# A second recorded plan for attention, first weights split one stage early, and step-size products moved ahead of the last K tiles

## The chip, the cores and the metric

The kernel runs on one core of a Trainium2 chip. The metric is the device time of one execution in microseconds. A core has five engines with a queue each: TensorE (PE, matmuls; its weight loads are shown as PEld), VectorE (DVE), ScalarE (ACT), GpSimd (POOL) and SyncE (SP), which here only issues DMAs. Each engine runs its own queue of instructions in order, and engines wait for one another by semaphores.

## The reference

One layer of a hybrid decoder on 256 tokens (b = 1, s = 256) of width 2048, all in float32. Cut to what matters:

```python
a_in = _rmsnorm(h, attn_norm_g[i])
proj = a_in @ w_in[i]
z, xbc, dt_raw, q, k, v = jnp.split(proj, [o1, o2, o3, o4, o5], axis=-1)
xbc = jax.nn.silu(_causal_dwconv(xbc, conv_w[i], conv_b[i]))
xs, bm, cm = jnp.split(xbc, [...], axis=-1)
dt = jax.nn.softplus(dt_raw + dt_bias[i])
y = _ssd(xs_h, dt, a_neg, bm, cm)          # chunked state-space scan, 32 heads of 64, 4 groups
...
y_ssm = _rmsnorm(y * silu(z), ssm_norm_g[i])
y_att = _swa_sinks(qh, kh, vh, sinks[i])   # 32 query heads, 8 key heads of 64, window 128, sinks
h = h + jnp.concatenate([y_ssm, y_att], axis=-1) @ w_out[i]
u = _causal_dwconv(_rmsnorm(h, ffn_norm_g[i]) @ w_up[i], ffn_conv_w[i], ffn_conv_b[i])
g_ff, u_ff = jnp.split(u, [D_FF], axis=-1)
h = h + (jax.nn.silu(g_ff) * u_ff) @ w_down[i]
gate = jax.nn.sigmoid(_rmsnorm(h, ple_norm_g[i]) @ w_ple_gate[i])
pe = _rmsnorm(p[i] @ w_ple_proj[i], ple_post_g[i])
h = h + gate * pe
```

## The kernel before

Every large product is made of float32 numbers split in two halves of the type fp32r: hi is the rounded number, lo the rest, and a product is hi*hi + hi*lo + lo*hi. A weight block of 128 x 1024 is loaded by SP into one of 7 raw buffers (`w`), cast by ScalarE to `wh` and subtracted by VectorE to `wl` (`split`, L580 to L584; 4 buffers of each). One such block makes a weight group on TensorE: 12 matmuls of 128 x 512 (2 token blocks x 2 K tiles x 3), into a pair of accumulators `acc`, one for each block of 128 tokens. There are two pairs; a pair can be written again once its reader, an evacuation by ScalarE or `add_to_h` on VectorE (L799, two adds into the residual `h`), has run.

The kernel has four parts:

- **First products** (about 5 to 54 us). For each of 16 K tiles, `first_products` (L732) multiplies the input with two columns of w_in into `acc_b` and `acc_c` (the B and C of the scan), and `dt_products` (L738, L739) adds the step sizes into a bank `ms`. TensorE's order is written by hand. The last two K tiles go column by column, and the step-size products of the last four K tiles stand behind them. The weights of the step sizes (`dhl`) lie in a pool that closes here; the next part uses its space.
- **SSD part** (about 55 to 325 us). A `Recorder` records each instruction with its reads, writes and buffer rings, gives it a duration from a table of costs (`cost`), and a list scheduler (`solve`, six rounds) sets the order on all five engines, which are then issued in that order. All these instructions show the line L280. `x0` to `x3` are the four groups of heads; for each, TensorE forms `ms<-Xd,seg` (within a chunk), `ms<-xe,Bt` (states) and `ms<-prev,CT` (from the state before) between weight groups. `acc_b`, `acc_c` and `dt` enter with given times at which they are taken to be ready.
- **Attention** (about 325 to 600 us). TensorE's order is written by hand: a table `at` says at which weight group (slot) a step is put between the products. The other four engines are ordered by the general tile scheduler, which a few `high_priority` blocks steer. For each of four groups of query heads: evacuate q (L1148), normalise and rotate it, turn it by a DMA transpose, scores (L1221) into `sc`, mask add (L1225), maximum (L1232, L1234), exponentials with their sum (L1237, L1241), `den` (L1242, L1243), scaling (L1246 or L1248), a copy to `half` (L1250), a DMA transpose to `flip` (L1171), GpSimd's copy back to `s` (L1172), values (L1264) into `tr`, and their split to `yh`, `yl`. Three such chains run per group: the first token block at once, the second in two halves. In between run the output products of the SSD groups and of the query groups before, with their `add_to_h`.
- **FFN and gate** (about 600 to 1402 us). A planner of its own (`Plan`) orders all engines. Its first products are those of the layer embedding with four blocks of `w_pe`.

Of the kernel before, what the change touches and what calls it, by code (L numbers as in the profile page):

```python
# [21 lines left out]
P = 128  # L22
T = 256
# [26 lines left out]
GATES_SECOND = (1, 3)  # L50
TURNED = ("by", "xby", "xby", "xby")
# [24 lines left out]
class Ring:  # L76

    def __init__(self, n, at=()):
        self.n, self.at, self.frees = n, at, []
# [17 lines left out]
class Plan:  # L97
# [3 lines left out]
    def __init__(self):  # L101
        self.jobs = []
# [9 lines left out]
    def run(self):  # L112
# [37 lines left out]
        for j in self.jobs:  # L150
            j.ready = j.at
            idle.setdefault(j.engine, 0.0 if j.engine == "PE" else -20.0)
            if not j.need:
                waiting.setdefault(j.engine, []).append(j)
# [95 lines left out]
class Recorder(Plan):  # L250

    def __init__(self, engines, tables):
        super().__init__()
        self.tables, self.open, self.rings = tables, None, {}
        self.V, self.S, self.G, self.PE, self.SY = (Voice(self, *e) for e in engines)
# [4 lines left out]
    def ring(self, pool, tag, n, at=()):  # L260
        return self.rings.setdefault((id(pool), tag), Ring(n, at))

    def keep(self, real, shape, pool=None, tag=None, n=1, at=-20.0):
        t = Lazy(shape, F32, None, real=real)
# [52 lines left out]
    def solve(self, idle, rounds=6):  # L317
        before = [list(j.after) for j in self.jobs]
        pe = [j for j in self.jobs if j.engine == "PE"]
        best = None  # L320
        for _ in range(rounds):
            done = self.simulate(pe, idle, before)
            end = max(j.start + j.dur for j in done if j.engine == "PE")
            if best is None or end < best[0]:
                best = end, done, {j: (j.start, j.late, j.ready) for j in done}
            pe = [j for j in done if j.engine == "PE"]
        self.end = best[0]
        for j in best[1]:
            j.start, j.late, j.ready = best[2][j]
        return best[1]  # L330

    def simulate(self, pe, idle, before):
        for j, a in zip(self.jobs, before):
            j.after = list(a)
            j.late, j.then, j.ready = math.inf, [], j.at
            for r, i in j.slots:
                if i >= r.n:
                    j.after.extend(k for k in r.frees[i - r.n] if k is not j)
                elif r.at:
                    j.ready = max(j.ready, r.at[i])  # L340
# [74 lines left out]
def cost(engine, method, args, kw, outs, ins):  # L415
# [21 lines left out]
    return 0.07 + 0.00107 * n, 0.0  # L437
# [3 lines left out]
def hybrid_layer(  # L441
# [279 lines left out]
    with xin_:  # L721
# [21 lines left out]
        for k in range(KT):  # L743
# [86 lines left out]
    with tc.tile_pool(name="ssd", bufs=1) as sp, tc.tile_pool(name="dram", bufs=1, space=bass.MemoryType.DRAM) as dp:  # L830
        plan = Recorder(zip(("DVE", "ACT", "POOL", "PE", "SP"), real_engines), {AF.Silu, AF.Exp, AF.Ln, AF.Sin})
# [260 lines left out]
        for step in ORDER:  # L1092
# [13 lines left out]
        jobs = plan.solve({"PE": 0.0, "ACT": -4.0, "DVE": -3.0, "POOL": -3.0, "SP": -20.0})  # L1106
# [4 lines left out]
        keys_acc = [t.real() for t in keys_acc]  # L1111
        for lhs, *_ in held.values():
            lhs.t = [(h.real(), l.real()) for h, l in lhs.t]
    sb, (acc_pair, tr_tile, ms_tile), hres, pe_group = eager, real_tiles, real_h, ExitStack
    fill(const)
    by_hand.__exit__(None, None, None)
# [3 lines left out]
    ssh = sb(small, [P, NB, 4], "ssh", bufs=1)  # L1120
    with tc.tile_pool(name="att_s", bufs=2) as as_, tc.tile_pool(name="att", bufs=2, reuse_waits="tile") as ap_, tc.tile_pool(name="ps_sc", bufs=1, space=PSUM) as ps_sc:
        qscaled = sb(as_, [P, HD], "qgs", bufs=1)
# [43 lines left out]
        def flipped(dst, n, put):  # L1166
# [4 lines left out]
            nc.sync.dma_start_transpose(flip, half.rearrange("p a n -> p (a n)"))  # L1171
# [38 lines left out]
        def scores(j, b, kvs):  # L1210
# [5 lines left out]
            sc = ps_sc.tile([P, 2, 2 * NC // (2 * W), W], F32, tag="sc", name=nm("sc"))  # L1216
            for kv in kvs:
                for i in range(2):
                    for e in range(2):
                        es = slice(e * HD, (e + 1) * HD)  # L1220
                        PE.matmul(  # L1221
                            sc[:, e, (kv - kvs[0]) * 2 + i, :], lhsT=qT[es, kv * 2 + i, :], rhs=kT[es, 2 * j + kv, :W], start=True, stop=True
                        )
# [9 lines left out]
            with tc.high_priority():  # L1233
                V.tensor_tensor(out=v3(nm_, 2), in0=v3(nm_, 2), in1=pairs(nsink), op=ALU.min)  # L1234
# [4 lines left out]
            with tc.high_priority():  # L1239
                V.tensor_tensor(out=v3(es_, 2), in0=v3(nm_, 2), in1=pairs(sink), op=ALU.add)  # L1240
                S.activation(out=es_, in_=es_, func=AF.Exp)  # L1241
                V.tensor_tensor(out=den, in0=den, in1=es_, op=ALU.add)  # L1242
                V.reciprocal(den, den)  # L1243
# [10 lines left out]
        def values(j):  # L1254

            yT = Lhs(yp_, KG, "y")
            for b in range(NB):
                o = tr_tile()
                for kv in range(2):
                    pT = probs.pop((j, b, kv))  # L1260
                    vs = slice((2 * j + kv) * HD, (2 * j + kv + 1) * HD)
                    for kb in range(b + 1):
                        for e in range(2):
                            PE.matmul(  # L1264
                                v3(o[e * HD : (e + 1) * HD, kv * 2 * P : (kv + 1) * 2 * P], 2),
                                lhsT=v[kb][:, vs],
                                rhs=pT[e][:, :, kb, :],
                                start=(kb == 0),
                                stop=(kb == b),
                                skip_group_check=True,  # L1270
                            )
# [36 lines left out]
        def embedding():  # L1308
            pt_ = sb(act, [P, KG, T], "ah3")[:, :KW, :]
            nc.scalar.dma_start(pt_, pT)  # L1310
            nc.scalar.dma_start(fcw, ffn_cw)
# [8 lines left out]
        with tc.manual_schedule(engines={PE.engine}):  # L1320
            for part in (
                lambda: q(0),
                lambda: chunk(11, load_v),
                lambda: q(1),
                lambda: output(1),
                lambda: q(2),
                lambda: output(2),
                lambda: q(3),
                *(lambda i=i: output(i) for i in range(3, 8)),
            ):  # L1330
                for _ in part():
                    if slot in at:
                        at[slot]()
                    slot += 1
        fill(as_)
    mix.close()
# [9 lines left out]
    with tc.tile_pool(name="ffn", bufs=2, reuse_waits="tile") as fp:  # L1346

        plan = Plan()
# [116 lines left out]
        def embed(n, ks):  # L1465
            w = weights(w_pe[n, 0])
# [590 lines left out]
```

## Time and profile before

| what | us |
|---|---|
| time, median of 3 runs (lowest, highest) | 1403.42 (1402.94, 1405.18) |
| time of the profiled execution | 1403.67 |
| its span from first to last instruction | 1402.0 |
| TensorE busy in the span | 1387.4 |
| VectorE busy | 1222.8 |
| ScalarE busy | 987.3 |
| GpSimd busy | 129.1 |
| mean granted clock of TensorE (share) | 0.996 |

The profile lists groups of instructions with busy time, mean duration, and the idle time of the engine in front of them with the instruction that ended it. A row of the timeline has the start, the duration, the engine, the line, the operation, output <- inputs, how many alike follow each other, and in brackets the idle time before the row and what ended it. A wait for several semaphores is put down to the one that came last by the profile, which need not be the one that mattered. Matmuls overlap, so the duration of one (0.39 us) is more than the distance to the next (0.23 us).

### The profile page before, as it was taken

How to read it: one execution, taken by the hardware profiler on the slowest of the kernel's cores; microseconds unless marked ns; L12 is line 12 of the kernel's file. 1: busy time of each engine (PE TensorE's matmuls, PEld its weight loads, DVE VectorE, ACT ScalarE, POOL GpSimd, SP SyncE). 2: the span in 40 equal slices, each digit the busy share in tenths (PEclk: the TensorE clock that was granted, in tenths of full speed). 3: DMA queues.
4: the chain of work that ended last, by engine and by line, in shares of the span. 5: the costliest groups of instructions: out<-in, count | busy, mean ns of one | idle time of the engine just before them, and what ended most of it. 6: DMA issues, size and time to landing. Idle time of an engine off the chain costs nothing.

```text
span 1402.0 us, 18224 instructions
## 1 busy us (share of the span) xinstructions
PE 1387.4 (99%) x6307; PEld 1134.1 (81%) x6307; DVE 1222.8 (87%) x1641; ACT 987.3 (70%) x1302; POOL 129.1 (9%) x113
## 2 busy tenths in 40 slices
PE   9999999999999999999999999999999999999998
PEld 7787888888776777888888888888888888888886
DVE  5698877767679898699999999999999999987998
ACT  6687686774666767476787785867687676877763
POOL 0010100018155251000000000000000000000000
PEclk9999999999999999999999999999999999999999
DMA  9576777767686787676887786786877677788563
GB/s 337 211 243 196 210 235 218 206 192 226 182 216 179 213 227 192 203 228 192 253 234 205 228 212 210 206 255 192 232 213 225 214 219 228 198 251 274 169 202 105
DMA packets 189292, 302.57 MB, mean 216 GB/s; under 512 B 116561, under 2 KB 119185, under 8 KB 188945
## 3 DMA queue, kind: packets, MB, share of 16 engines
q1 hardware_dynamic: 188768, 300.95, 72.1%
q8 instruction: 49, 0.80, 0.2%
q10 hardware_dynamic: 432, 0.48, 0.1%
q14 instruction: 43, 0.34, 0.1%
HBM read 270.41 MB, written 4.23 MB: 196 GB/s over the span
## 4 chain that ended last, share of the span: by engine, by line
PE 65%; DVE 1%; DMA 0%; issue 0%; ACT 0%; POOL 0%; DVEq 0%; SPq 0%; POOLq 0%; ACTq 0%
PE b L1433 19%; PE b L1431 19%; PE b L1432 19%; PE acc L620 3%; PE acc L621 2%; PE acc L622 2%; PE tr L1264 1%; PE b L1528 0%; DMA flip<-half 0%; PE sc L1221 0%; DVE wl L584 0%; DVE h L799 0%; PE b L1978 0%; DVE nm L1234 0%; DVE c L1939 0%
## 5 line engine op out<-in xcount | busy, mean ns | idle before, releaser
L1385 ACT CAST wh<-w 128x1024 fp32r<-128x1024 f32 x300 | 314.2, 1052 | 153.3 <-PE b L1433 115.8
L1389 DVE TENSOR_TENSOR wl<-w,wh 128x1024 fp32r<-128x1024 f32 x300 | 361.5, 1220 | 27.4 <-ACT wh L1385 24.9
L584 DVE TENSOR_TENSOR wl<-w,wh 128x1024 fp32r<-128x1024 f32 (+1 forms) x115 | 148.3, 1296 | 55.4 <-ACT wh L583 55.0
L583 ACT CAST wh<-w 128x1024 fp32r<-128x1024 f32 (+1 forms) x115 | 116.6, 1026 | 73.1 <-PE acc L622 61.7
L1431 PE MATMUL b<-wh,gh 128*128 128x512 f32 x398 | 155.0, 389 | 0.0
L1433 PE MATMUL b<-wh,gl 128*128 128x512 f32 x398 | 154.9, 389 | 0.0
L1432 PE MATMUL b<-wl,gh 128*128 128x512 f32 x398 | 154.8, 389 | 0.0
L1433 PE MATMUL b<-wh,al 128*128 128x512 f32 x360 | 140.1, 389 | 0.0
L1431 PE MATMUL b<-wh,ph 128*128 128x512 f32 x352 | 137.2, 390 | 0.0
L1433 PE MATMUL b<-wh,pl 128*128 128x512 f32 x352 | 137.0, 389 | 0.0
L1432 PE MATMUL b<-wl,ph 128*128 128x512 f32 x352 | 136.9, 389 | 0.0
L1431 PE MATMUL b<-wh,ah 128*128 128x512 f32 x344 | 134.0, 390 | 0.0
L1432 PE MATMUL b<-wl,ah 128*128 128x512 f32 x344 | 133.8, 389 | 0.0
L280 DVE TENSOR_TENSOR wl<-w,wh 128x1024 fp32r<-128x1024 f32 x80 | 97.4, 1235 | 29.4 <-ACT wh L280 26.4
L280 PE MATMUL acc<-wh,ah 128*128 128x512 f32 x288 | 116.6, 405 | 0.0
L280 ACT CAST wh<-w 128x1024 fp32r<-128x1024 f32 x80 | 82.9, 1048 | 46.3 <-PE acc L280 42.0
L280 PE MATMUL acc<-wh,al 128*128 128x512 f32 x288 | 112.5, 391 | 0.0
L280 PE MATMUL acc<-wl,ah 128*128 128x512 f32 x288 | 112.4, 390 | 0.0
L620 PE MATMUL acc<-wh,yh 128*128 128x512 f32 x224 | 89.7, 401 | 3.4 <-ACT s L1246 1.9
L621 PE MATMUL acc<-wl,yh 128*128 128x512 f32 x224 | 88.0, 393 | 0.0
L622 PE MATMUL acc<-wh,yl 128*128 128x512 f32 x224 | 87.9, 393 | 0.0
L1433 PEld LDWEIGHTS b<-wh,gl 128*128 128x128 f32 x398 | 74.7, 188 | 15.5
(297 smaller groups left out, 2855.4 us busy)
## 6 DMA issues: line engine op xcount, KB each, us to landing
w<-in_w_up_dram SPq DMA_DIRECT2D x176, 512.0 KB, 4.2
w<-in_w_in_dram SPq DMA_DIRECT2D x126, 512.0 KB, 4.4
w<-in_w_down_dram SPq DMA_DIRECT2D x88, 512.0 KB, 4.4
w<-in_w_out_dram SPq DMA_DIRECT2D x64, 512.0 KB, 4.2
w<-in_w_pg_dram SPq DMA_DIRECT2D x32, 512.0 KB, 3.8
seg<-scr SPq DMA_DIRECT2D x8, 512.0 KB, 6.1
xt<-in_xT_dram SPq DMA_DIRECT2D x16, 128.0 KB, 6.6
h<-in_x_dram SPq DMA_DIRECT2D x2, 1024.0 KB, 8.7
```

The source lines that it names most:

```text
L280: getattr(real, method)(*(concrete(a) for a in args), **{k: concrete(a) for k, a in kw.items()})
L583: S.copy(hi, src)
L584: V.tensor_tensor(out=lo, in0=src, in1=hi.bitcast(F32), op=ALU.subtract)
L620: PE.matmul(acc[b], lhsT=hi, rhs=wh[:, i, :], start=(k == 0), stop=False)
L621: PE.matmul(acc[b], lhsT=hi, rhs=wl[:, i, :], start=False, stop=False)
L622: PE.matmul(acc[b], lhsT=lo, rhs=wh[:, i, :], start=False, stop=(k == total - 1 or (b == NB - 1 and k + 1 == whole)))
L1264: PE.matmul(v3(o[e * HD : (e + 1) * HD, kv * 2 * P : (kv + 1) * 2 * P], 2), lhsT=v[kb][:, vs], rhs=pT[e][:, :, kb, :], start=(kb == 0), st ...
L1385: S.copy(o.h, src.t)
L1389: V.tensor_tensor(out=o.l, in0=src.t, in1=o.h.bitcast(F32), op=ALU.subtract)
L1431: PE.matmul(t, lhsT=hi, rhs=wh, start=first, stop=False)
L1432: PE.matmul(t, lhsT=hi, rhs=wl, start=False, stop=False)
L1433: PE.matmul(t, lhsT=lo, rhs=wh, start=False, stop=last)
```

## The change

1. The step-size products of the last four K tiles now stand ahead of the column-by-column products of the last two.
2. Attention is recorded as well, in a second `Recorder` with the table set {Exp}. Its plan is handed the state of the first one: when each engine comes to rest, and when the buffers of each ring come free (`carry`, `left`, `begun`). The `high_priority` blocks are gone, scores and values become groups on TensorE, the transposes and two loads of ScalarE go through the plan. The FFN's planner starts from the times at which attention's engines come to rest.
3. The first three splits of attention's first weights are made at the end of the SSD list (`AHEAD = 3`), and the four splits of `w_pe` at the end of the attention list.
4. The costs of the plan change: GpSimd's power, two-input and other operations, a ScalarE DMA issue, and a floor of 0.25 for small VectorE operations. `acc_b`, `acc_c` and `dt` are taken to be ready at -2.5, 0.2 and -5.0 instead of -4.4, -1.6 and 0.3.

TensorE, VectorE, GpSimd and SP have the same instructions in another order; ScalarE has one table load more, in the SSD part. TensorE's order in attention and in the FFN is the same as before.

```diff
+AHEAD = 3
...
+        for k in range(KT - 4, KT):
+            dt_products(k)
         for c in range(KW):
             for k in (KT - 2, KT - 1):
                 first_products(k, c)
-        for k in range(KT - 4, KT):
-            dt_products(k)
         by_hand.close()
...
+    if engine == "ACT" and method == "dma_start":
+        return 0.1, 4.0
...
     if engine == "POOL":
-        return 0.4 + 0.0012 * n, 0.0
+        if kw.get("op") == ALU.pow:
+            return 0.6 + 0.16 * n, 0.0
+        return (0.6 + 0.0015 * n if method == "tensor_tensor" else 0.3 + 0.0011 * n), 0.0
...
-    return 0.07 + 0.00107 * n, 0.0
+    return max(0.07 + 0.00107 * n, 0.25 if n <= 8 else 0.0), 0.0
...
-        acc_b, acc_c = ([plan.keep(t, [P, NC], ps_acc, f"acc{b}", 2, at) for b, t in enumerate(acc)] for acc, at in ((acc_b, -4.4), (acc_c, -1.6)))
+        acc_b, acc_c = ([plan.keep(t, [P, NC], ps_acc, f"acc{b}", 2, at) for b, t in enumerate(acc)] for acc, at in ((acc_b, -2.5), (acc_c, 0.2)))
...
-        dt_ps = plan.keep(dt_ps, [P, NC], ps_ms, "ms", 2, 0.3)
+        dt_ps = plan.keep(dt_ps, [P, NC], ps_ms, "ms", 2, -5.0)
...
                 keys_acc = in_chunk(10)
+                early = [load_w(w_in[12, s]) for s in range(AHEAD)]
...
+        plan = Recorder(zip(("DVE", "ACT", "POOL", "PE", "SP"), real_engines), {AF.Exp}, before.rest, before)
+        V, S, G, PE, SY = plan.V, plan.S, plan.G, plan.PE, plan.SY
+        keys_acc = [plan.carry(t, (ps_acc, f"acc{b}")) for b, t in enumerate(keys_acc)]
...
+        early = [tuple(plan.carry(t, (wp, f"w{e}"), F32R) for e, t in zip("hl", ts)) for ts in early]
...
-            nc.sync.dma_start_transpose(flip, half.rearrange("p a n -> p (a n)"))
+            SY.dma_start_transpose(flip, half.rearrange("p a n -> p (a n)"))
...
-            with tc.high_priority():
-                V.tensor_tensor(out=v3(nm_, 2), in0=v3(nm_, 2), in1=pairs(nsink), op=ALU.min)
+            V.tensor_tensor(out=v3(nm_, 2), in0=v3(nm_, 2), in1=pairs(nsink), op=ALU.min)
...
-                products(acc, aT, load_w(w_in[c, s]), s * KW, KW, KT, s == n - 1)
+                products(acc, aT, early.pop(0) if early else load_w(w_in[c, s]), s * KW, KW, KT, s == n - 1)
...
-        with tc.manual_schedule(engines={PE.engine}):
...
+        early = [load_w(w_pe[n, 0]) for n in range(KG)]
+        jobs = plan.solve()
...
+        early = [(h.real(), l.real()) for h, l in early]
...
-        plan = Plan()
+        plan = Plan(before.rest)
...
-            w = weights(w_pe[n, 0])
+            w = Box()
+            w.slot, w.jobs = splits.take(), []
+            w.h, w.l = early[n]
```

Where it moves instructions, at three places. First TensorE at the end of the first products, before: the last products of the last two K tiles, then the eight step-size matmuls (`ms<-...,dhl`), then the first transposes of the SSD part.

```order
L732 MATMUL acc_33_160<-wl_526,ah_26_153 128x512
L732 MATMUL acc_34_161<-wl_526,ah_26_153 128x512
L738 MATMUL ms_164<-ah_26_153,dhl_163 64x256
L739 MATMUL ms_164<-al_27_154,dhl_163 32x256
...
L280 MATMUL tr_618<-ident_120,ct_110_591 128x128
```

And in the change (L756 is `first_products`, L762 and L763 are `dt_products`, L298 is the recorded plan):

```order
L762 MATMUL ms_164<-ah_26_153,dhl_163 64x256
L763 MATMUL ms_164<-al_27_154,dhl_163 32x256
L756 MATMUL acc_31_158<-wh_515,ah_26_153 128x512
L756 MATMUL acc_32_159<-wh_515,ah_26_153 128x512
...
L756 MATMUL acc_34_161<-wl_526,ah_26_153 128x512
L298 MATMUL tr_613<-ident_120,ct_114_599 128x128
```

The eight matmuls moved past the 24 products of the last two K tiles; between them and the first transposes now stand 12 matmuls into `acc_b` (31, 32) and 12 into `acc_c` (33, 34).

Second TensorE in the SSD part at x0, before: the weight groups are `acc<-wh,...`, one row stands here for the ends of each.

```order
L280 MATMUL acc_223_1141<-wh_1076,al_21_148 128x512
L280 MATMUL ms_1166<-Xd_219_1131,seg_942 128x64 x8
L280 MATMUL ms_1181<-xe_1160,Bt_859 128x512
L280 MATMUL acc_222_1137<-wh_1107,ah_20_147 128x512
...
L280 MATMUL acc_223_1141<-wh_1107,al_21_148 128x512
L280 MATMUL ms_1212<-Xd_232_1175,seg_970 128x64 x8
L280 MATMUL ms_1225<-prev_1203,CT_708 128x512
```

And in the change:

```order
L298 MATMUL acc_220_1135<-wh_1078,al_21_148 128x512
L298 MATMUL acc_219_1131<-wh_1094,ah_20_147 128x512
...
L298 MATMUL acc_220_1135<-wh_1094,al_21_148 128x512
L298 MATMUL ms_1184<-xe_1178,Bt_864 128x512
L298 MATMUL ms_1189<-Xd_223_1149,seg_970 128x64 x8
L298 MATMUL ms_1206<-Xd_226_1155,seg_991 128x64 x8
L298 MATMUL ms_1220<-prev_1200,CT_706 128x512
```

The first token block's `ms<-Xd,seg` and `ms<-xe,Bt` moved one weight group later and changed places; all four now stand together. In the same way x3's first `ms<-Xd,seg` and `ms<-xe,Bt` moved one weight group earlier.

Third VectorE in attention, in the second group of query heads, around its second token block's first half, beside the values of the first group: before, `den` (the sum of exponentials), the two `yl` of the values, then the adds into `h` that free accumulators.

```order
L584 TENSOR_TENSOR wl_4047<-w_4044,wh_4046 128x1024
L1242 TENSOR_TENSOR den_3830<-den_3830,es_3835 128x4
L584 TENSOR_TENSOR yl_829_3934<-tr_3935,yh_828_3933 128x4x128
L584 TENSOR_TENSOR yl_829_3934<-tr_3942,yh_828_3933 128x4x128
L1243 RECIPROCAL den_3830<-den_3830 128x4
L799 TENSOR_TENSOR h_1_83<-h_1_83,acc_823_3913 128x512
L799 TENSOR_TENSOR h_2_84<-h_2_84,acc_824_3914 128x512
```

And in the change:

```order
L298 TENSOR_TENSOR wl_3919<-w_3741,wh_3915 128x1024
L298 TENSOR_REDUCE ss_829_3938<-hsq_3917 128x8
L298 TENSOR_SCALAR rs_t_3943<-ss_829_3938 128x8
L298 TENSOR_TENSOR h_1_83<-h_1_83,acc_812_3869 128x512
L298 TENSOR_TENSOR h_2_84<-h_2_84,acc_813_3873 128x512
L298 TENSOR_TENSOR qkr_3883<-qkr_3883,rs_832_3945 128x512
L298 TENSOR_TENSOR wl_3972<-w_3759,wh_3966 128x1024
L298 TENSOR_TENSOR den_3933<-den_3933,es_3911 128x4
L298 RECIPROCAL den_3933<-den_3933 128x4
```

The two adds now stand ahead of `den`; the `yl` moved far behind it.

ScalarE at the same place, before: exponentials of the second block's first half, casts of weights (`wh`) and of the values (`yh`), the scaling by `den`, the copy to `half`.

```order
L1237 ACTIVATE s_793_3820,den_3830<-s_793_3820,nm_3827 128x256 x4
L583 CAST wh_4046<-w_4044 128x1024
L1241 ACTIVATE es_3835<-es_3835 128x4
L583 CAST yh_828_3933<-tr_3935 128x4x128
L583 CAST yh_828_3933<-tr_3942 128x4x128
L1246 ACTIVATE s_793_3820<-s_793_3820,den_3830 128x256 x4
L583 CAST wh_4064<-w_4062 128x1024
L1250 COPY half_3844<-s_793_3820 128x2048
```

And in the change:

```order
L298 ACTIVATE s_809_3858,den_3933<-s_809_3858,nm_3888 128x256 x4
L298 ACTIVATE es_3911<-es_3911 128x4
L298 ACTIVATE hsq_3963<-qkr_3886 128x512
L298 CAST wh_3966<-w_3759 128x1024
L298 CAST yh_837_3970<-tr_3897 128x4x128
L298 CAST yh_837_3970<-tr_3902 128x4x128
L298 CAST wh_3982<-w_3803 128x1024
L298 ACTIVATE s_809_3858<-s_809_3858,den_3933 128x256 x4
L298 COPY half_4019<-s_809_3858 128x2048
```

The cast that stood behind the scaling now stands ahead of it.

More of the change, by code (lines that the diff above doesn't have):

```diff
@@ L76, with __init__ @@
 class Ring:
-    def __init__(self, n, at=()):
-        self.n, self.at, self.frees = n, at, []
+    def __init__(self, n, at=(), begun=0):
+        self.n, self.at, self.frees, self.begun = n, at, [[] for _ in range(begun)], begun
     def take(self):
@@ L151, in run @@
             j.ready = j.at
-            idle.setdefault(j.engine, 0.0 if j.engine == "PE" else -20.0)
+            idle.setdefault(j.engine, self.rest[j.engine] if self.rest else 0.0 if j.engine == "PE" else -20.0)
             if not j.need:
@@ L260, in ring, with left, carry, keep @@
     def ring(self, pool, tag, n, at=()):
-        return self.rings.setdefault((id(pool), tag), Ring(n, at))
-    def keep(self, real, shape, pool=None, tag=None, n=1, at=-20.0):
-        t = Lazy(shape, F32, None, real=real)
+        key = (id(pool), tag)
+        if key not in self.rings:
+            old = self.before and self.before.rings.get(key)
+            if old and len(old.frees) >= n:
+                self.rings[key] = Ring(n, [self.before.left(js) for js in old.frees[-n:]], n)
+            else:
+                self.rings[key] = Ring(n, at, n if at else 0)
+        return self.rings[key]
+    def left(self, jobs):
+        return max((j.start + j.dur + j.lag - self.end for j in jobs), default=-20.0)
+    def carry(self, v, key, dtype=F32):
+        old, i = v.tile.slot
+        ring_ = self.ring(*key, old.n)
+        t = Lazy(v.tile.shape, dtype, None, (ring_, i - len(old.frees) + old.n), v.tile.real)
+        t.at = self.before.left([u[0] for u in v.tile.uses if u[3]])
+        return View.whole(t)
+    def keep(self, real, shape, pool=None, tag=None, n=1, at=-20.0, dtype=F32):
+        t = Lazy(shape, dtype, None, real=real)
         t.at = at
@@ L315, in use, with solve @@
         t.uses = keep
-    def solve(self, idle, rounds=6):
+    def solve(self, rounds=6):
+        idle = self.idle
         before = [list(j.after) for j in self.jobs]
@@ L329, in solve @@
             j.start, j.late, j.ready = best[2][j]
+        self.rest = {e: max((j.start + j.dur for j in best[1] if j.engine == e), default=-20.0) - self.end for e in idle}
         return best[1]
@@ L1215, in scores @@
             s = sb(ap_, [P, 2 * m, W], f"s{b}", bufs=2 + b)
[L1216 to L1223, printed above, removed]
+            shape = [P, 2, 2 * NC // (2 * W), W]
+            sc = plan.tile(ps_sc, shape, "sc", lambda: ps_sc.tile(shape, F32, tag="sc", name=nm("sc")), 1)
+            with pe_group():
+                for kv in kvs:
+                    for i in range(2):
+                        for e in range(2):
+                            es = slice(e * HD, (e + 1) * HD)
+                            PE.matmul(
+                                sc[:, e, (kv - kvs[0]) * 2 + i, :], lhsT=qT[es, kv * 2 + i, :], rhs=kT[es, 2 * j + kv, :W], start=True, stop=True
+                            )
             sc = sc.rearrange("p e m w -> p (e m) w")
@@ L1238, in scores @@
             es_ = sb(as_, [P, 2 * m], "es")
[L1239 to L1243, printed above, removed]
+            V.tensor_tensor(out=v3(es_, 2), in0=v3(nm_, 2), in1=pairs(sink), op=ALU.add)
+            S.activation(out=es_, in_=es_, func=AF.Exp)
+            V.tensor_tensor(out=den, in0=den, in1=es_, op=ALU.add)
+            V.reciprocal(den, den)
             if b:
@@ L1319, in hybrid_layer @@
         slot = KT // KW
-        with tc.manual_schedule(engines={PE.engine}):
[L1321 to L1334, printed above, removed]
+        for part in (
+            lambda: q(0),
+            lambda: chunk(11, load_v),
+            lambda: q(1),
+            lambda: output(1),
+            lambda: q(2),
+            lambda: output(2),
+            lambda: q(3),
+            *(lambda i=i: output(i) for i in range(3, 8)),
+        ):
+            for _ in part():
+                if slot in at:
+                    at[slot]()
+                slot += 1
+        early = [load_w(w_pe[n, 0]) for n in range(KG)]
+        jobs = plan.solve()
+        V, S, G, PE, SY = real_engines
+        for job in jobs:
+            job.fn()
+        em = [t.real() for t in em]
+        early = [(h.real(), l.real()) for h, l in early]
+        before = plan
+        sb = eager
         fill(as_)
+    hres = real_h
+    by_hand.__exit__(None, None, None)
     mix.close()
```

64 lines of the change are left out of this document (33 added, 31 removed).

## The prediction

> **What bounds the kernel now.** I read the page's span and engine lines first, then TensorE's busy time in 50 us stretches, then what it waited for, then the timeline around each wait.
>
> ```profile
> span 1402.0 us, 18224 instructions
> ...
> PE 1387.4 (99%) x6307; PEld 1134.1 (81%) x6307; DVE 1222.8 (87%) x1641; ACT 987.3 (70%) x1302; POOL 129.1 (9%) x113
> ```
>
> TensorE is the bound: 1387.4 of 1402.0 us. The change removes no matmul (it moves some), so all it can win is within TensorE's 14.6 us of idle time and what the matmuls behind a stall lose. Where the idle time lies (columns: stretch, its length, then busy time and starts of PE, PEld, DVE, ACT, POOL, granted clock, DMA share, GB/s):
>
> ```profile
> 50.00:100.00 50.00, 48.85 (x233) 39.76 (x233) 44.42 (x116) 40.95 (x55) 3.24 (x2) 1.00 0.59 186
> 100.00:150.00 50.00, 48.56 (x223) 39.36 (x222) 41.52 (x52) 40.01 (x51) 5.72 (x5) 0.97 0.76 222
> ...
> 300.00:350.00 50.00, 50.00 (x222) 41.43 (x221) 37.09 (x50) 27.56 (x34) 32.53 (x27) 1.00 0.73 223
> 350.00:400.00 50.00, 49.73 (x235) 39.74 (x234) 38.08 (x47) 31.12 (x62) 20.16 (x18) 1.00 0.65 183
> 400.00:450.00 50.00, 47.09 (x225) 35.83 (x224) 37.28 (x44) 31.86 (x57) 19.66 (x15) 0.97 0.79 198
> 450.00:500.00 50.00, 49.03 (x240) 37.67 (x239) 44.21 (x53) 35.68 (x71) 21.73 (x19) 1.00 0.78 218
> ...
> 600.00:650.00 50.00, 50.00 (x238) 41.72 (x237) 47.12 (x72) 35.63 (x53) 0.71 (x1) 1.00 0.68 217
> 1350.00:1402.00 52.00, 45.40 (x206) 37.63 (x205) 45.49 (x62) 23.21 (x27) 0.00 (x0) 0.96 0.37 130
> ```
>
> The last stretch's 6.60 us is untouched by the change. Within reach are 1.15 and 1.44 us at the start of the SSD part and 0.27 + 2.91 + 0.97 = 4.15 us in attention. The two switches, from SSD to attention and from attention to the FFN, lie in 300 to 350 and 600 to 650: TensorE is busy there for all 50 us. What ended the waits (total us, times, longest):
>
> ```profile
> PE acc L620 <- DVE h L799: 2.0, 5, 0.7
> PE acc L620 <- ACT s L1246: 1.9, 1, 1.9
> PE ms L280 <- DVE Xd L280: 1.4, 1, 1.4
> ...
> PE tr L280 <- issue: 0.8, 1, 0.8
> ...
> PE tr L280 <- ACT ct L280: 0.2, 1, 0.2
> ```
>
> A stall costs more than its idle time, in two ways:
>
> ```profile
> 435.80 0.39 PE L621 MATMUL acc<-wl,yh 128*128 128x512 f32 x1
> ...
> 436.03 0.39 PE L622 MATMUL acc<-wh,yl 128*128 128x512 f32 x1
> ...
> 438.31 0.47 PE L620 MATMUL acc<-wh,yh 128*128 128x512 f32 x1 [1.89 <-ACT s L1246]
> ```
> ```profile
> 110.94:114.10 3.16, 3.16 (x8) 0.52 1.11 289
> 438.35:441.90 3.55, 3.55 (x9) 0.56 0.00 0
> 448.00:451.00 3.00, 3.00 (x15) 1.00 0.99 265
> ```
>
> First, matmuls start 0.23 us apart but each lasts 0.39, so a stall takes 0.16 us beyond its idle time. Second, in the 3.16 us after the stall of 1.44 us the granted clock is 0.52, and in the 3.55 us after that of 1.89 it is 0.56; that loses 3.16 x 0.48 = 1.5 and 3.55 x 0.44 = 1.6 us. After the stall of 0.70 us at 447.56 the clock stays 1.00.
>
> So the prices are: end of the first products 1.0 + 0.2 = 1.2; x0's stall 1.44 + 0.16 + 1.5 = 3.1; attention 4.15 idle + 7 stalls x 0.16 + 1.6 = 6.9. Together 11.2 us is the most that these edits can return.
>
> By the Trainium skill, "TensorE: Matmul & The Clock Gate", Part 1, the half clock comes only after an idle window of about 3.4 us; stalls under 2 us would then slow nothing, the 3.1 us of slow matmuls would stay wherever the stalls went, and the sum below would be about 6 us. The two rows of 0.52 and 0.56 right behind such short stalls speak against that, so I count the slow matmuls with their stalls.
>
> **The change part by part.** *The last step-size products.*
>
> ```profile
> 54.57 1.27 ACT L280 ACTIVATE ct<-acc,rx 128x512 f32<-128x512 f32 x2 [10.42 <-PE ms L739]
> 54.57 0.17 DVE L280 CAST posf<-posi 128x2 f32<-128x2 int32 x1 [11.47 <-PE ms L739]
> ```
>
> Both engines sat idle over 10 us until the last of these products, though acc_b was complete 12 matmuls x 0.23 = 2.8 us before the products began. In the new order 24 matmuls (24 x 0.23 = 5.5 us) come behind them, so ScalarE can evacuate acc_b (1.27 us) inside the last 12, and the transposes have their input when TensorE is there. I take the whole 1.2 us; bounds 0 and 1.2. VectorE also starts up to 5 us earlier.
>
> *x0's stall.*
>
> ```profile
> 108.98 0.69 DVE L280 TENSOR_TENSOR xe<-Xd,dec 128x512 f32<-128x512 f32 x1
> ...
> 109.09 1.97 PE L280 MATMUL ms<-Xd,seg 128*128 128x64 f32 x16 [1.44 <-DVE Xd L280]
> ```
>
> TensorE was ready at 109.09 - 1.44 = 107.65. It now does one more weight group first (12 x 0.23 = 2.8) and arrives 1.2 earlier: 109.2. It then wants xe, which ended at 109.67 before. So VectorE has to be 0.5 us ahead of its old times. It was idle for 5.6 of the 50 us from 50 to 100, and 4.6 of these (50 to 54.57) are the wait that goes; behind it VectorE runs nearly without a gap, so it carries an earlier start along as far as TensorE's products let it. I take 1.5 of the 5 us. The stall goes with its slow matmuls, and I leave 0.3 for the other first products that moved (x3's stand one group earlier): 2.8, bounds 0 and 3.1.
>
> *Attention.*
>
> ```profile
> 432.00 1.03 ACT L583 CAST wh<-w 128x1024 fp32r<-128x1024 f32 x1
> ```
> ```profile
> 421.04 0.17 DVE L1242 TENSOR_TENSOR den<-den,es 128x8 f32<-128x8 f32 x1 [2.02 <-ACT s L1237]
> ...
> 422.62 4.30 DVE L584 TENSOR_TENSOR wl<-w,wh 128x1024 fp32r<-128x1024 f32 x2
> ...
> 433.93 2.37 POOL L1172 COPY s<-flip 128x2048 uint16<-128x2048 uint16 x1 [9.22 <-DMA flip<-half]
> ...
> 434.20 2.11 DVE L1242 TENSOR_TENSOR den<-den,es 128x4 f32<-128x4 f32 x1
> ...
> 437.52 1.25 DVE L799 TENSOR_TENSOR h<-h,acc 128x512 f32<-128x512 f32 x2
> ```
> ```profile
> 446.84 0.67 DVE L799 TENSOR_TENSOR h<-h,acc 128x512 f32<-128x512 f32 x1
> ...
> 447.56 0.50 PE L620 MATMUL acc<-wh,yh 128*128 128x512 f32 x1 [0.70 <-DVE h L799]
> ...
> 455.33 0.15 DVE L1242 TENSOR_TENSOR den<-den,es 128x4 f32<-128x4 f32 x1
> ```
>
> The stall at 438.31 is put down to ScalarE, but the first matmul there opens a new pair of accumulators, and its weights were cast from 432.00 on. What ended just before it was the first of the two h adds at 437.52 (half of 1.25 us), which frees that pair. The adds were late since they stood behind den, two yl and a reciprocal, and den took 2.11 us instead of the 0.15 of 455.33 because GpSimd's copy ran beside it. The new order has the adds ahead of den. From den at 421.04 its VectorE queue to the adds is den 0.17, reciprocal 0.20, scaling 1.23, maximum 1.22, 0.15, wl 1.22, 0.17, wl 1.22, sum of squares 0.68, 0.17: 6.4 us. Two casts now stand among the exponentials ahead of den (2.0 us more), and one GpSimd copy will stretch the queue by the 1.9 us that 422.62's pair (4.30 for 2 x 1.22) shows. 421.0 + 2.0 + 6.4 + 1.9 + 1.25 = 432.6, and TensorE wants the pair at 436.03 + 0.23 = 436.26: 3.7 us to spare. That stall (1.89 + 0.16 + 1.6 = 3.7) goes. The next pair's adds follow 8 VectorE instructions later, about 5.5 us and another stretched copy: 432.6 + 5.5 + 1.9 + 0.65 = 440.7 for the first, against 441.7 when TensorE is there; this one may stay in part. The rest of the attention stalls are h adds of under 0.7 us each; I expect half of their 3.2 us. So 3.7 + 1.6 = 5.3, bounds from the rival below to 6.9.
>
> *Early splits.* The first three splits of attention and the four of the FFN's first products were already made while TensorE was busy (300 to 350 and 600 to 650: 0 idle), so I cost them at 0 gain. They now sit at the end of the list ahead, where VectorE has 37.09 and ScalarE 27.56 of 50 us, so nothing waits for them; if that cover were gone, a cast and a wl, 1.03 + 1.22 us, would stand before a product once.
>
> *Costs of the plan, DMAs.*
>
> ```profile
> L280 ACT ACT_TABLE_LOAD x13 | 16.7, 1283 | 2.6 <-DVE xc L280 2.1 <-DVE BT L280 0.4
> ```
>
> One table load is added in the SSD part, 1.28 us on an engine busy 40 of 50 us: 0, at worst 1.3. SP's and GpSimd's instructions are the same in number; the transposes stand elsewhere among the weight loads (the two of q group 0's second block are now next to each other, with weight loads queued behind them), and of ScalarE's two loads one is issued later. What SP's order can cost is rival (b). The FFN's own order hardly moves: 0, bounds -1 and 1.
>
> Sum: 1.2 + 2.8 + 5.3 = 9.3 us. The profiled execution took 1403.67, the median is 1403.42; from the median it gives **1394.1 us**.
>
> **The rivals.**
>
> (a) *Attention keeps its stalls elsewhere.* The plan has no term for VectorE held by GpSimd, and GpSimd is busy 20 of each 50 us here. For it: den at 0.15 and at 2.11 us. Against it: 3.7 us to spare where it hurt most. If half of the 5.3 is lost again: 1403.4 - 1.2 - 2.8 - 2.6 = about 1397 (1399.4 if all of it is).
>
> (b) *A new stall at the values products,* the case that ends slower.
>
> ```profile
> 422.26 2.44 POOL L1172 COPY s<-flip 128x2048 uint16<-128x2048 uint16 x1 [4.61 <-DMA flip<-half]
> ```
> ```profile
> 423.90 2.81 PE L1264 MATMUL tr<-s,v 128*64 128x256 f32 x24
> ```
>
> GpSimd's last copy ended at 424.70; its readers are the last 8 of 24 matmuls, from 423.90 + 16 x 0.1 = 425.5: 0.8 us to spare. In the new order ScalarE's copy to half for that block stands behind one cast more (1.03 us), and SP issues both transposes of the block in a row, each of which takes 5.1 us from issue to landing:
>
> ```profile
> flip<-half SPq DMA_TRANSPOSE x66, 5.1
> ```
>
> If the second one is late by half of that, TensorE idles 2.5 - 0.8 = 1.7 us and the half clock follows: 1.7 + 0.16 + 1.5 = 3.4 per q group; if by all of it, 4.3 + 0.16 + 1.6 = 6.1. For four groups that is 13.6 to 24.4. With the old stalls gone (6.9) and 4.0 won in the SSD part: 1403.4 - 10.9 + 13.6 = 1406 to 1417. It decides from 10.9 / 4 = 2.7 us per group. Against it: only the first group is so tight in the order; the others have the pair apart.
>
> (c) *The SSD plan only trades its stall.* x3's first products stand one group (2.8 us) earlier. A stall there of x0's size costs 3.1 and takes x0's gain back: 1403.4 - 1.2 - 5.3 + 0.3 = about 1397.
>
> (d) *The attention plan does nothing for time,* since TensorE's order is the same there: 1403.4 - 4.0 = 1399.4.
>
> **How the numbers follow.** The forecast (1391 to 1397) has 0.50, (a) 0.15, (c) 0.07, (d) 0.10, (b) 0.13 (0.09 of it over 1406), and 0.05 stay for what I don't see, half of it faster. A measurement of this kernel can tell about 0.2% (2.8 us) from no change, so faster means under 1400.6: 0.50 + 0.15 + 0.07 + 0.04 (of (d), whose 1399.4 is near the bound) + 0.02 = 0.78. Slower, above 1406.2: 0.09. The same: 0.13. The range 1390.5 to 1402.5 takes in the forecast, (a), (c) and (d), 0.82 with the ends of the bounds, and leaves out (b).
>
> **What would show it.** TensorE idle from 50 to 100 at 0 to 0.2 us (first step); no row under 0.9 of the clock at 107 to 115 and 436 to 445, and no wait on Xd or xe over 0.5 us (second and third); the h adds in pairs, over 2 us before the products that reopen their banks; idle in 400 to 500 of about 1.5 instead of 3.9. I am wrong if the values products show a wait on GpSimd's copy, if the slow clock turns up at another place, or if idle time appears in the FFN.

## The result, and the profile after

| | us |
|---|---|
| before, median of 4 runs (lowest, highest) | 1403.61 (1402.94, 1405.18) |
| changed, median of 4 runs (lowest, highest) | 1390.20 (1389.99, 1390.74) |
| ratio, with its 95% interval | 0.9903 (0.9886 to 0.9921) |
| profiled execution of the changed kernel, its span | 1389.99, 1388.3 |

The change saves 13.4 us. 1394.1 was forecast, with a range from 1390.5; the time lies 0.3 us below it. The page's first lines and the view of waits of TensorE, of the changed kernel:

```profile
span 1388.3 us, 18219 instructions
...
PE 1380.9 (99%) x6307; PEld 1133.9 (82%) x6307; DVE 1224.0 (88%) x1641; ACT 989.9 (71%) x1303; POOL 125.7 (9%) x113
```
```profile
PE ms L568 <- PEq L2091: 0.8, 1, 0.8
```

That is the whole list of waits. The one left belongs to the first microseconds and was there before. The stretches of 50 us (columns as in the prediction):

```profile
0.00:50.00 50.00, 49.16 (x223) 38.58 (x224) 30.13 (x48) 31.03 (x43) 2.71 (x12) 1.00 0.91 336
50.00:100.00 50.00, 49.98 (x237) 41.12 (x236) 45.34 (x116) 41.58 (x55) 2.92 (x2) 1.00 0.70 208
100.00:150.00 50.00, 50.00 (x249) 41.47 (x248) 43.58 (x56) 41.55 (x54) 3.98 (x4) 1.00 0.70 210
...
350.00:400.00 50.00, 50.00 (x237) 40.34 (x236) 39.75 (x50) 32.84 (x65) 14.46 (x14) 1.00 0.67 190
400.00:450.00 50.00, 50.00 (x259) 39.27 (x257) 44.61 (x51) 39.98 (x72) 23.92 (x19) 1.00 0.80 217
450.00:500.00 50.00, 50.00 (x239) 39.53 (x236) 45.52 (x54) 35.50 (x70) 22.16 (x18) 1.00 0.76 216
...
1350.00:1388.30 38.30, 31.72 (x146) 26.35 (x144) 31.91 (x46) 14.01 (x16) 0.00 (x0) 0.95 0.35 121
```

In attention TensorE is busy without a gap where it idled 4.15 us, and the granted clock is 1.00 in all of these stretches but the last, whose idle time is the same 6.6 us as before. Where the time came from is best read from the starts of one and the same matmul in the two timelines, since that counts idle time, slow matmuls and the restart together:

| TensorE has reached | before | changed | lead | gained on the way |
|---|---|---|---|---|
| one of the step-size products | 47.86 | 46.84 | 1.02 | 1.02, first products |
| the transposes of the SSD part | 56.17 | 53.69 | 2.48 | 1.46, the gap behind the step-size products |
| a product late in the SSD part | 284.59 | 278.78 | 5.81 | 3.33, x0 |
| a product early in attention | 381.04 | 375.23 | 5.81 | 0 |
| an early product of the FFN | 612.47 | 598.79 | 13.68 | 7.87, attention |

Behind it the lead stays 13.7. The lead of 1.0 in the first products was not in the prediction at all.

### The profile page after: what moved, and what is told of

Read it like the earlier page. It is cut to its first block, busy times and chain, and to the rows that moved or that the text cites. A ratio compares the mean times of both kernels' runs of the same rounds, so it can differ in the third digit from the quotient of the medians.

```text
span 1388.3 us, 18219 instructions
## 1 busy us (share of the span) xinstructions
PE 1380.9 (99%) x6307; PEld 1133.9 (82%) x6307; DVE 1224.0 (88%) x1641; ACT 989.9 (71%) x1303; POOL 125.7 (9%) x113
## 4 chain that ended last, share of the span: by engine, by line
PE 99%; DVE 0%; DVEq 0%; issue 0%
PE acc L298 35%; PE b L1473 19%; PE b L1475 19%; PE b L1474 19%; PE acc L756 3%; PE ms L298 2%; PE tr L298 1%; PE sc L298 1%; PE b L1572 1%; PE ms L568 0%; PE ms L763 0%; PE ms L762 0%; PE b L2022 0%; DVE c L1983 0%; DVE c L1984 0%; DVE c L1973 0%
## 5 line engine op out<-in xcount | busy, mean ns | idle before, releaser
L1427 ACT CAST wh<-w 128x1024 fp32r<-128x1024 f32 x296 | 309.9, 1052 | 145.8 <-PE b L1475 108.0
L1431 DVE TENSOR_TENSOR wl<-w,wh 128x1024 fp32r<-128x1024 f32 x296 | 356.6, 1219 | 22.7 <-ACT wh L1427 20.1
L298 DVE TENSOR_TENSOR wl<-w,wh 128x1024 fp32r<-128x1024 f32 x180 | 244.6, 1368 | 79.3 <-ACT wh L298 77.3
L298 ACT CAST wh<-w 128x1024 fp32r<-128x1024 f32 x180 | 188.0, 1049 | 138.3 <-PE acc L298 122.0
L298 PE MATMUL acc<-wh,ah 128*128 128x512 f32 x448 | 178.8, 399 | 0.0
L298 PE MATMUL acc<-wh,al 128*128 128x512 f32 x448 | 174.8, 390 | 0.0
L298 PE MATMUL acc<-wl,ah 128*128 128x512 f32 x448 | 174.6, 390 | 0.0
L298 PE MATMUL acc<-wh,yh 128*128 128x512 f32 x256 | 101.0, 395 | 0.0
L298 PEld LDWEIGHTS acc<-wh,ah 128*128 128x128 f32 x448 | 84.2, 188 | 19.5 <-issue 2.1
L298 PE MATMUL acc<-wl,yh 128*128 128x512 f32 x256 | 99.9, 390 | 0.0
L298 PE MATMUL acc<-wh,yl 128*128 128x512 f32 x256 | 99.7, 389 | 0.0
L298 PEld LDWEIGHTS acc<-wl,ah 128*128 128x128 f32 x448 | 84.2, 188 | 18.2 <-issue 1.4
L298 PEld LDWEIGHTS acc<-wh,al 128*128 128x128 f32 x448 | 84.1, 188 | 17.7
```

The lines of the kernel that those rows point to most:

```text
L298: getattr(real, method)(*(concrete(a) for a in args), **{k: concrete(a) for k, a in kw.items()})
L1427: S.copy(o.h, src.t)
L1431: V.tensor_tensor(out=o.l, in0=src.t, in1=o.h.bitcast(F32), op=ALU.subtract)
```

## The experiments

Each is the kernel before or the changed one with the edit shown or named. Times are medians. The kernel before was timed again in each set of runs, with medians from 1402.19 to 1403.61, so a time is set beside the one of its own set where that matters; a ratio is to that one, with its 95% interval. "By the starts" means as in the table above, in the profiled executions.

### Was it the load at the head of ScalarE's queue?

In the changed kernel the 176 KB load of `fcw`, which the tile scheduler had put at 1.5 us, goes out at 302 us. The first products wait for loads, so it could be the 1.0 us.

e1, the kernel before with that load moved:

```diff
     by_hand.__enter__()
+    nc.scalar.dma_start(fcw, ffn_cw)
...
-            nc.scalar.dma_start(fcw, ffn_cw)
```

> The kernel before, with the one 176 KB load of the FFN's convolution weights (fcw) moved from the head of ScalarE's queue (1.55 us) to the start of the SSD part. Theory A, the load takes DMA time from the first weight blocks, whose DMA engines are full from 5 to 50 us: 176 KB at about 350 KB per us is 0.5 us, paid once or twice, so 0.5 to 1.0 us faster (1402.6 to 1403.1), and TensorE is busy for all of 5 to 10 us and of 30 to 35 us. Theory B, the difference of 1.0 us in the first products is chance of one execution: no change, 1403.6.

Measured: 1403.16 beside 1403.01, ratio 1.0002 (0.9993 to 1.0012). Here TensorE was 0.6 us earlier at the same matmul (47.25 instead of 47.86), but the total is no shorter.

e2, the changed kernel with the load put back:

```diff
     fcw = sb(const, [P, 88 * 4], "fcw")
+    nc.scalar.dma_start(fcw, ffn_cw)
...
-            S.dma_start(fcw, ffn_cw)
```

> The changed kernel with only that load put back to the head of ScalarE's queue. Theory A: 0.5 to 1.0 us slower than the changed kernel, 1390.7 to 1391.2, with the idle time of the first products back. Theory B: 1390.2.

Measured: 1390.83. That could be either theory, with the changed kernel timed in another set of runs, so both were run again side by side.

> The changed kernel once more, beside the next one on the same chip: 1390.2, the base for it.

> The changed kernel with the fcw load at the head of ScalarE's queue, as in e2, now beside the changed kernel on one chip. Theory A, the load delays the first weight blocks: TensorE's 36th matmul starts at 11.4 to 11.7 us instead of 10.5 to 11.1, and the time is 0.5 to 1.0 us over the changed kernel's. Theory B, what it delays is made up again while the first products wait for other loads: the times are within 0.3.

Measured: 1390.56 (1390.44 to 1390.89) for the changed kernel, 1390.33 (1390.17 to 1390.48) with the load early. The load costs nothing that these runs can tell. In a0, which loads late, the matmul that the expectations call TensorE's 36th started at 11.71 us, about as late as in the runs with the load early (11.44 to 11.73); in the other runs that load late it started at 10.53 to 11.57. The start of the matmul of 46.84 lies between 46.45 and 48.47 in the profiles with the load late and between 47.26 and 48.66 in those with it early. **The lead of 1.02 in the first products lies within this scatter of single executions,** and of the 13.68 us, 12.7 belong to the change: in a0 the first products give 0.12, and the stretches behind them give 1.46, 3.32 and 7.87.

### The step-size products

e3, the kernel before with only these moved:

```diff
+        for k in range(KT - 4, KT):
+            dt_products(k)
         for c in range(KW):
             for k in (KT - 2, KT - 1):
                 first_products(k, c)
-        for k in range(KT - 4, KT):
-            dt_products(k)
```

> The kernel before with only the step-size products moved. Theory A, VectorE's earlier start at 49 us is carried along to x0: the gap at the end of the first products (1.4 us) goes and x0's stall with its slow matmuls (3.4 to 3.6 us from start to start) too, 1398.6 to 1399. Theory B, x0's stall hangs on the place of its products in TensorE's order, which is as before here: only 1.4 us, 1402.2, and a wait on Xd of 1 us or more stays.

Measured: 1399.06 beside 1403.01, ratio 0.9966 (0.9954 to 0.9979): eight matmuls moved by 5.5 us save 4 us, theory A's time. From its timeline and its windows (PE only):

```profile
107.31 1.97 PE L280 MATMUL ms<-Xd,seg 128*128 128x64 f32 x16 [0.72 <-DVE Xd L280]
```
```profile
107.00:110.50 3.50, 3.19 (x21) 1.00 1.15 264
```

The gap at 55 us is gone. x0's products are at their old place in TensorE's order, and TensorE arrives there earlier (106.59 instead of 107.65); still the stall is 0.72 instead of 1.44, and no half clock follows. So theory A holds in the main: VectorE carries its earlier start (49.9 us there) along for over 50 us. By the starts the gap gives 1.46 us and the stretch with x0 2.68 of the changed kernel's 3.33. In this execution attention took 2.0 us less too, though the order of VectorE, ScalarE and GpSimd there is the old one: the stall of 438 us did not come. So it depends on what happens to run side by side and not on the order alone; two `wl` in that queue took 2.35 us (at 418.51) where they took 4.30 before (at 422.62).

e4, the changed kernel with only these put back:

> The changed kernel with only the step-size products put back behind the last two K tiles (the plan still takes its inputs to be ready early). Theory A: the gap of 1.2 to 1.4 us is back and x0 stalls too, 1394 to 1395. Theory B: only the gap is back, 1391.6, since x0's products stand one weight group later.

Measured: 1393.19, 0.9926 (0.9914 to 0.9939), 3.0 us over the changed kernel: between the two theories. Its waits:

```profile
PE ms L298 <- DVE adt L298: 1.1, 1, 1.1
...
PE tr L298 <- issue: 0.8, 1, 0.8
PE tr L298 <- ACT ct L298: 0.2, 1, 0.2
```

The gap is back, and VectorE's lateness shows at another place, `adt` at 81 us, not at x0, which the new order has put one weight group later and which TensorE reaches later here by that stall. By the starts the stretch with x0 gives 2.2 us with the later place alone, 2.7 (e3) with the earlier start alone and 3.3 with both: either remedy does most of it.

### The two plans apart

e6, the kernel before with the step-size products, the new costs and the new ready times, attention as before:

> The kernel before with the step-size products moved, the new costs and the new ready times, and attention as before. Theory A, the two parts add up: 4.9 us faster (5.9 in the changed kernel up to the end of the SSD part, less 1.0 for fcw, which stays at the head here), 1398.7, with the attention waits as before. Theory B, part of the attention's stalls came from the state that the SSD part leaves: under 1398.

Measured: 1399.03 beside 1402.2, 0.9977 (0.9968 to 0.9986). No wait is left between 8 and 380 us in its timeline, and by the starts it gains 1.46 + 3.34 us there, theory A's 4.9 but for 0.1. But attention waits as before and took 0.9 us more in this execution, and by the medians e6 saves 3.2 us, no more than e3 does without the new plan.

e7, the changed kernel with the SSD part as before:

> The changed kernel with the SSD part as before: step-size products behind, old ready times, old costs in the first plan; attention is recorded with the new costs. Theory A, parts add up: 7.8 us of attention and 1.0 of fcw faster, 1394.8, with x0's stall and the gap at 55 us still there and no wait in attention. Theory B: attention's gain needs the earlier SSD end, over 1396.

Measured: 1395.73, 0.9955 (0.9940 to 0.9970), between the two theories. Its waits:

```profile
PE ms L299 <- DVE Xd L299: 1.4, 1, 1.4
PE acc L759 <- ACT wh L610: 1.2, 1, 1.2
...
PE tr L299 <- issue: 0.8, 1, 0.8
PE tr L299 <- ACT ct L299: 0.2, 1, 0.2
```

x0's stall and the gap are there as before, nothing in attention, and a wait of 1.2 us in the first products, where the waits differ from one execution to the next. By the starts attention gains 7.87 us, as in the changed kernel: it does not need the earlier end of the SSD part, and theory A holds. By the starts the parts also add up: 1.46 + 3.34 from e6 and 7.87 from e7 are 12.67, and the changed kernel gains 12.66. The medians add up less well: 3.2 and 6.5 us are 9.6 before rounding, where the changed kernel without its early splits (e5 below, same set) saves 11.7. The 0.9 us of e6 and the 1.2 us of e7 would fill that, but which executions had them is not known.

### The early splits

e5, the changed kernel without them:

```diff
-AHEAD = 3
+AHEAD = 0
...
-        early = [load_w(w_pe[n, 0]) for n in range(KG)]
...
-            w = Box()
-            w.slot, w.jobs = splits.take(), []
-            w.h, w.l = early[n]
+            w = weights(w_pe[n, 0])
```

> The changed kernel without the early splits: attention's and the FFN's first weights are split in their own plans again. Theory A, the switches showed TensorE busy without them, so they buy nothing: 1390.2 within 0.5. Theory B, the second plan needs them, since its weights cannot be asked for before it starts: a cast and a wl (1.03 + 1.22 us) stand before a product at one or both switches, 1392 to 1396 with the slow clock.

Measured: 1390.47 (1390.03 to 1390.74) beside 1402.2, and no wait but the first in its view. They buy nothing, as forecast.

### The table of costs

e9, the changed kernel with the old table:

> The changed kernel with the old table of costs in both plans. Theory A, it is the recorded order that removes the stalls, whose slack (over 3 us at the adds into h) is larger than the changes in the costs (under 1 us for most operations): 1390.2 to 1391. Theory B, the costs carry it: GpSimd's power was planned at 0.4 us where the trace shows 1.65, so waits on qkr and qT come back, 1392 or more.

Measured: 1395.99, 0.9956 (0.9941 to 0.9970). It gives back 5.5 us beside e5 of the same set. By the starts attention takes 6.6 us longer than in the changed kernel and the gap and the SSD part take the same:

```profile
PE acc L298 <- DVE h L298: 3.2, 2, 2.9
PE sc L298 <- DVE s L298: 1.0, 1, 1.0
```

So recording attention is not enough by itself; theory A falls. Theory B has the time but not the place: no wait on qkr or qT stands in this view. Which entry it is was tried with two halves of the new table.

c1, the old table with only GpSimd's power at its new cost:

```diff
+        if kw.get("op") == ALU.pow:
+            return 0.6 + 0.16 * n, 0.0
         return 0.4 + 0.0012 * n, 0.0
```

> The changed kernel with the old table of costs, except for GpSimd's power, which is planned at the new 1.88 us instead of 0.41 (1.65 in the traces). Theory A, the power's cost is what the old table got wrong: 1390.2 to 1391, no wait on the adds into h. Theory B, it is the sum of the small ones (the copies, the floor of 0.25 for small VectorE operations): 1393 or more.

c2, the new table with only GpSimd's old costs:

> The changed kernel with only GpSimd's old costs, the rest of the table new. Theory A: the waits of the old table are back, 1394 to 1396. Theory B: 1390 to 1392.

Measured: 1391.60 (one wait of 1.1 us on an add into `h` is left, beside one of 1.0 us in the first products) and 1390.36 (none). GpSimd's costs are not needed, and the power's cost alone removes most of the waits as well. Neither theory names the entry: with either half the scheduler finds an order that holds, in c1 but for that one wait, and only the old table as a whole leads to one that doesn't. Whether the floor of 0.25 us alone would do, without the entry for ScalarE's loads, was not tried.

### Which wait was it at 438 us?

The view of waits named ScalarE's scaling; the prediction said that TensorE waited for the adds into `h`. d1 and d2 take the changed kernel, where that wait is gone, and put only this one pair of adds later in VectorE's queue, by six and by eight instructions:

```diff
         jobs = plan.solve()
+        dve = [j for j in jobs if j.engine == "DVE"]
+        anchor = dve[dve.index(held_back[1]) + 6]
+        jobs = [j for j in jobs if j not in held_back]
+        at_ = jobs.index(anchor) + 1
+        jobs[at_:at_] = held_back
```

> The changed kernel with one pair of adds into h (second SSD output, first column block) put six VectorE instructions later in its queue, behind den and two wl. Theory A, the adds free the accumulators that TensorE opens at 429.8 us: the first would end at about 430.9, so TensorE stalls about 1 us there, idle 0.9, and the time is 1391.3 with a full clock or 1392.8 if the half clock follows. Theory B, the wait at this place was on ScalarE's scaling, as the view of waits has it for the kernel before: no stall, 1390.2.

> The same pair put eight VectorE instructions later, behind rs_t and the mask add too: the first add ends at about 433. Theory A: TensorE idles about 3 us there and runs at half clock for some 3 us behind it: 3.0 + 0.2 + 1.5 = 4.7 us, 1394.9. Theory B: no stall, 1390.2. If the half clock came only after an idle window of 3.4 us, 1393.4.

Measured: 1391.21 and 1395.24 beside 1402.19, theory A's times. By the starts attention takes 1.00 and 4.73 us longer than in the changed kernel. VectorE and TensorE in d1's timeline:

```profile
429.87 1.27 DVE L298 TENSOR_TENSOR h<-h,acc 128x512 f32<-128x512 f32 x2
```
```profile
430.69 0.47 PE L298 MATMUL acc<-wh,yh 128*128 128x512 f32 x1 [0.72 <-ACT half L298]
```

And in d2's, with its windows:

```profile
432.84 2.46 DVE L298 TENSOR_TENSOR h<-h,acc 128x512 f32<-128x512 f32 x4
```
```profile
433.65 0.47 PE L298 MATMUL acc<-wh,yh 128*128 128x512 f32 x1 [2.82 <-DVE h L298]
```
```profile
433.60:436.90 3.30, 3.25 (x9) 0.63 1.17 268
437.00:440.00 3.00, 3.00 (x13) 0.85 0.53 138
```

Moving two adds makes TensorE stall at this product, in both, each time 0.8 us behind the start of the first add. In d1 the profile puts the stall down to ScalarE's copy to `half`, which was not touched and which the product doesn't read. In the changed kernel that copy ran until 430.66 as well, and TensorE opened the pair at 429.88 without a wait:

```profile
428.76 1.90 ACT L298 COPY half<-s 128x2048 uint16<-128x2048 uint16 x1
```
```profile
429.88 0.39 PE L298 MATMUL acc<-wh,yh 128*128 128x512 f32 x1
```

So the label is false, and the one at 438.31 before most likely too: there the first add had started at 437.52, 0.8 us ahead, and it is 0.8 us again in e1 and e6, whose views name ScalarE's scaling as well. The other stalls on adds in attention were not tested in this way.

## Why the prediction came out as it did

**The bound.** Right: all of the gain is TensorE's waits and the slow matmuls behind them, the tail is the same.

**The step-size products: 1.2 forecast, 1.46 measured** (in e4 the same stretch takes 1.47 longer again). Right, but the price counted one restart of 0.16 where the gap has two stalls (0.82 and 0.23 us). The lead that they give VectorE was right too: e3 shows it at x0.

**x0: 2.8 forecast, 3.33 measured.** Right in mechanism: e3 and e4 show that the earlier start and the later place each remove most of it. The price of 3.1 was 0.2 low: the granted clock is 0.50 for 3.41 us (111.08 to 114.49), which loses 1.7 and not 1.5. The 0.3 left for the other first products was not needed.

**Attention: 5.3 forecast, 7.87 measured. This is the term that was mis-sized,** while the mechanism, adds into `h` that come late, was right. Two steps failed: the price of the stalls and the 1.6 us left for those that would stay.

First, its price of 6.9 us was too low. It counted idle time, 0.16 per stall and 1.6 for one half clock; the starts of the matmuls give 7.87. The half clock loses 1.7 us here too (0.50 for 3.41 us, 438.76 to 442.17). And behind a stall the next matmul also starts later: 0.31 instead of 0.23 behind 430.69 in d1 (431.00 follows), up to 0.34 in the kernel before. With 1.7, and 0.25 instead of 0.16 for each of seven stalls, the price is 7.6; the last 0.3 is not assigned.

Second, 1.6 us were left for h adds that would still come late, and none did. The walk along VectorE's queue had the first pair done at 432.6 in the time of the kernel before, with 3.7 us to spare. In the changed kernel:

```profile
415.10 0.15 DVE L298 TENSOR_TENSOR den<-den,es 128x8 f32<-128x8 f32 x1
...
421.97 0.69 DVE L298 TENSOR_TENSOR h<-h,acc 128x512 f32<-128x512 f32 x1 [0.23 <-PE acc L298]
423.35 0.69 DVE L298 TENSOR_TENSOR h<-h,acc 128x512 f32<-128x512 f32 x1 [0.70 <-PE acc L298]
```

VectorE waits here for TensorE: each add runs as soon as its product has ended, and TensorE opens the bank again at 429.88, 7 us later. From den to the first add it takes 6.9 us (6.4 in the walk). What the walk had too much of is the start (den ran at 415.10 + 6.38 = 421.5 in the old time, TensorE's lead being 6.38 here, not at 423.0: its last input was there before it in spite of the casts) and a GpSimd copy that fell into another stretch. The first add of the next pair, put at an end of 440.7, ended at 433.0, which is 439.4 in the old time.

**The range** had its lower end at 1390.5, under the most that the prices allowed (1403.4 - 11.2 = 1392.2). With 7.87 for 6.9, 3.33 for 3.1 and 1.46 for 1.2 the prices were 12.7, 1390.7. Whether the time falls just outside the range or just inside is chance (a0 took 1390.56). That the gain is 13.4 us, or 12.4 in a0 beside the kernel before of its set, and not 9.3, is not.

**Early splits: 0 forecast, 0 measured** (e5). **The FFN: 0, as forecast.** **The load that ScalarE issues later: 0** within what a0 and e2b can tell, though the first comparison looked otherwise.

**The costs of the plan** were taken to be covered by slack. That is right of the order that came out and wrong of the one that the old table would have given: e9 loses 5.5 us. The slack belongs to an order, not to a stage.

**The rivals.** (a) did not come about in the changed kernel, but is what e9 shows: TensorE waits 2.9 us for h adds behind two VectorE instructions that took 2.16 and 2.12 us instead of 0.16 and 1.2, beside copies by GpSimd:

```profile
438.02 2.16 DVE L298 TENSOR_TENSOR es<-nm,rows 128x4 f32<-128x4 f32 x1
440.11 2.12 DVE L298 TENSOR_TENSOR wl<-w,wh 128x1024 fp32r<-128x1024 f32 x1
...
442.75 1.27 DVE L298 TENSOR_TENSOR h<-h,acc 128x512 f32<-128x512 f32 x2
```
```profile
438.01 2.15 POOL L298 COPY s<-flip 128x2048 uint16<-128x2048 uint16 x1 [0.35 <-DMA flip<-half]
440.10 1.04 POOL L298 COPY half<-qkr 128x1024 uint16<-128x1024 uint16 x1
```

(b) did not come about:

```profile
408.86 5.23 POOL L298 COPY s<-flip 128x2048 uint16<-128x2048 uint16 x2 [7.47 <-DMA flip<-half]
```
```profile
417.52 2.81 PE L298 MATMUL tr<-s,v 128*64 128x256 f32 x24
```

Both copies ended at 414.09, 3.4 us before the first values product; the margin of 0.8 us, counted to the last 8 of the 24 as in the prediction, has grown to 5.0. (c) has no wait anywhere in the SSD part, and (d) falls with e7.

## What to carry to other kernels

Price a stall by the starts of the same instruction before and behind it, not by its idle time: here idle time and half clock gave 11.2 us, the starts 12.7. A name in a view of waits is a guess where a wait has several semaphores: move the suspected instruction alone, in its own queue, and see whether the stall comes. Where an order comes from a planner, a hand's walk along one queue gives its sign well and its slack poorly; leave the residual small if the walk finds spare time, and don't take the slack for a property of the stage when the planner's costs change.

## What the runs showed of the hardware

Whether matmuls run at half clock behind a stall is not set by the stall's length alone. Two long stalls of e6 in its timeline, and its windows around and behind them (PE only):

```profile
433.51 0.47 PE L624 MATMUL acc<-wh,yh 128*128 128x512 f32 x1 [2.40 <-ACT s L1250]
...
441.14 0.47 PE L624 MATMUL acc<-wh,yh 128*128 128x512 f32 x1 [1.50 <-DVE h L803]
```
```profile
433.00:436.50 3.50, 2.99 (x13) 1.00 0.00 0
...
440.00:443.50 3.50, 1.66 (x6) 1.00 1.13 200
443.50:447.00 3.50, 3.50 (x18) 1.00 1.07 303
```

Stalls of 2.40 and 1.50 us left the clock at 1.00 there, while 1.44 and 1.89 us before, 2.82 in d2 and 2.86 in e9 were each followed by 3.41 us at a clock of 0.50; over windows cut otherwise, as in the rows of the prediction and of d2, that reads as 0.52 to 0.63. No stall of 1.2 us or less was followed by it in any run. In the trace's record of the granted clock all changes lie whole multiples of 3.413 us apart: in the kernel before the stretches between them are 105.81 (31 times), 3.41, 324.27 (95 times), 3.41 and 955.73 us (280 times).

By the Trainium skill, "TensorE: Matmul & The Clock Gate", Part 1, the clock falls after an idle window of about 3.4 us, and the window is free-running. The multiples of 3.413 us agree with the second. With the first the stalls of 1.44 and 1.89 us do not agree, since neither fills such a window. Nor does the place in the window explain the difference, if the changes on record mark the windows: the stretch of 3.413 us that ended at 438.76 before was idle for 1.89 us and the half clock followed, the one from 431.60 to 435.01 in e6 was idle for 1.91 us and it did not. What decides is open.

The kernel with stalls scatters more. From the matmul of 381.04 to that of 612.47 attention took 229.40 to 232.30 us in the four profiles with the old attention (before, e1, e3, e6), and 223.56 us in all eight in which it has no wait. Over these runs the kernel before took 1399.5 to 1406.4 us in 46 executions, the changed one 1389.99 to 1390.89 in 8.
